# A hybrid decoder step on one core: the extra tokens' picks dealt on the core, and six expert blocks fetched into row buffers

## The chip, the cores and the metric

The kernel runs on one core of a Trainium2 chip. The metric is the device time of one execution in microseconds (us); the time of a kernel is the median of its runs. A core has five engines that run side by side, each with its own queue of instructions: TensorE (PE: matrix products, with its weight loads shown apart as PEld), VectorE (DVE), ScalarE (ACT), GpSimd (POOL) and SyncE (SP, which issues DMAs). Sixteen DMA engines move data between the memory and the on-chip SBUF. TensorE writes its results into PSUM, from which VectorE and ScalarE read.

## The reference, cut to what matters

One layer of a decoder for 272 prompt tokens (16 of them learned meta tokens) and 64 tokens of running sequences. First come a convolution branch and a state-space branch with a shared projection (the trunk). What the change touches is the expert mixer behind it:

```python
def peer_block(xb, w_q, keys, U, V):
    T = xb.shape[0]
    q = (xb @ w_q).reshape(T, PEER_HEADS, 2, D_KEY // 2)
    s = jnp.einsum('thcd,hckd->thck', q, keys).astype(jnp.float32)
    s1, i1 = lax.top_k(s[:, :, 0], PEER_TOPK)
    s2, i2 = lax.top_k(s[:, :, 1], PEER_TOPK)
    cand = (s1[..., :, None] + s2[..., None, :]).reshape(T, PEER_HEADS, PEER_TOPK * PEER_TOPK)
    sc, f = lax.top_k(cand, PEER_TOPK)
    ids = (jnp.take_along_axis(i1, f // PEER_TOPK, axis=-1) * N_KEYS
           + jnp.take_along_axis(i2, f % PEER_TOPK, axis=-1))
    g = jax.nn.softmax(sc, axis=-1)
    act = jax.nn.gelu(jnp.einsum('thkd,td->thk', U[ids], xb).astype(jnp.float32), approximate=False)
    w = (g * act).astype(xb.dtype)
    return jnp.einsum('thk,thkd->td', w, V[ids])
```

Every token picks 8 heads x 16 = 128 of 16384 experts; U and V hold 1024 numbers (4 KB) for each expert.

## The kernel before

**Three kinds of tokens.** 320 tokens go through the expert mixer (T2). 128 of them (NGAT) are "gathered": for each of their 128 picks, one indirect DMA of GpSimd fetches the picked rows of U and V for all 128 tokens at once (`gather`, L1150, 1 MB into a row buffer "wuv" of 2 x 1024 columns; there are UV = 5 such buffers), VectorE multiplies and sums (`pick_dot`, L1305), ScalarE applies the gelu and the pick's weight, and VectorE adds the weighted row of V to `ygat` (`pick_sum`, L1316). 184 tokens (ND) are "dense": their products with all experts are computed, and those that were not picked are masked out. The last 8 tokens (NX) are "extra": their 128 picks each are spread over the 128 partitions, 16 partitions to a token with 8 picks each, so that 8 further gathers serve all of them. That makes 136 gathers.

**The dense path.** U comes in 128 blocks of 512 KB. `u_block(b)` (L1416) multiplies block b with the dense tokens `nd` on TensorE (16 matmul records) and ScalarE writes the gelu into S (L1423). `g_step` (L1429) builds the mask with the weights as a product of two 0/1 matrices for 8 tokens at a time (L1449, through the two PSUM buffers "misc") and VectorE multiplies S by it (L1460). Then `v_block(b)` (L1520) multiplies the 128 blocks of V with S, and `finish` (L1496) and `finish_dense` (L1530) normalize and write the results.

**Stages and order.** The loop of the query phase (L1186) runs over 16 query halves j: a weight of w_q is loaded by SyncE (L273), cast on ScalarE (L243), its rest formed on GpSimd (L247), multiplied on TensorE (L176) and compared with the keys (L1199). Behind it run the U blocks and then the V blocks; a `Feed` hands out background tasks (picks, mask steps) at an even rate between the blocks. The framework places the instructions: each engine's order comes from a simulated schedule in which program order is the priority, so that U blocks can also fill gaps of the query phase. An engine then runs its own instructions strictly in that order, and so does SyncE with its DMA issues. Tiles of one tag in a pool share a fixed number of buffers; a new tile waits until an old one's last reader is done.

**How U blocks come in.** `fetch(i)` (L1179), called at j = 3 and j = 13, loads blocks 0 to 3 and 4 to 7 into eight places "pre" (PRE = 4 for each call). `bring` (L1386) loads the rest in order: into a ring of RING = 8 buffers of one block, which are the buffers that held the weights and their two parts before, and for blocks 16 to 23 (`again`, AGAIN = 24) into the places "pre" once more, each when the U block that was there is done. From block 24 on only the ring is left. Loads of odd blocks above LATE = 24 are issued by ScalarE, the others by SyncE (L1404). After block AGAIN - 1 the memory of the places becomes part of S (L1469).

**The extra tokens' picks.** Before, `place` (L1270) leaves ids and weights of the extra tokens in `xig`: a row for each token, which occurs in both halves of the partitions, and 64 columns (four heads) in each. `extra_columns` (L1293) deals them out by a round trip through memory: four small DMAs write `xig` to `xigd` (L1298, not before U block XW = 70 is done), a fifth reads it back as 8 columns on 128 partitions (L1301, not before block XR = 86), and VectorE copies the ids to `gid` and the weights to `ggw` (L1302, L1303). Their first use is the 65th gather.

Of the kernel before, what the change touches and what calls it, by code (L numbers as in the profile page):

```python
# [7 lines left out]
F32 = mybir.dt.float32  # L8
# [6 lines left out]
OP = mybir.AluOpType  # L15
AX = mybir.AxisListType

D = 1024
KD = 8
# [15 lines left out]
NK = 128  # L35
# [4 lines left out]
NX = 8  # L40
XQ = 128 // max(NX, 1)
ND = T2 - NGAT - NX
NPICK = 128
NCOL = NPICK + (NPICK // XQ if NX else 0)
# [8 lines left out]
SB = 84  # L53
SA = 29
PRE = 4
AGAIN = 24
HB = 64
KTILES = ((0, NGAT), (128, 128), (256, 64))
NU = (42, 26, 35)
# [4 lines left out]
RING = RB + 4  # L64
LATE = 24
OH = 2
UV = 5
# [3 lines left out]
XRES = 104  # L71
# [1 line left out]
PLACE = (42, 55)  # L73
LASTP = 126
XW = 70
XR = 86
RIGHT = "right"
TOPK = 16
EPS = 1e-6
# [38 lines left out]
def constants():  # L118
    c = np.zeros((128, NCST), np.float32)

    def put(name, a):
        o, n = CST[name]
        c[:a.shape[0], o:o + n] = a

    i = np.arange(128)
    put("ident", np.eye(128))
    put("tri", i[:, None] <= i[None, :])
    put("suf", i[:, None] > i[None, :])
    j, own, s = strips()
    n = np.arange(80)  # L130
    own = own[:, None]
    put("tri3", own & (s[j][:, None] == s[j][None, :]) & (j[:, None] <= j[None, :]))
    put("tri3n", own & (s[j][:, None] == s[None, :]) & (j[:, None] <= n[None, :]))
    put("suf3", own & (s[j][:, None] == s[j][None, :]) & (j[:, None] > j[None, :]))
    put("seg", own & (s[j][:, None] == np.arange(9)[None, :]))
    put("segs", own & (np.where(j < 64, j // 8 % 2, 2)[:, None] == np.arange(3)[None, :]))
    put("gsel", np.broadcast_to(np.arange(135) == 7, (128, 135)))
    for q in range(NQ):
        for t in range(TS):
            c[32 * (q % 4) + 8 * (q // 4) + t, CST["selq"][0] + 8 * q + t] = 1.0  # L140
    put("ones", np.ones((128, 128)))
    put("iota128", np.broadcast_to(np.arange(128), (128, 128)))
    put("sel32", i[:, None] % 32 == np.arange(32)[None, :])
    put("sel16", i[:, None] % 16 == np.arange(16)[None, :])
    put("sel8", i[:, None] % 8 == np.arange(8)[None, :])
    return c


def causal():
    m = np.zeros((128, T), np.float32)  # L150
    i, n = np.arange(128), np.arange(80)
    j, own, s = strips()
    m[:, 256:] = np.where(own[:, None] & (s[j][:, None] == s[None, :]) & (j[:, None] <= n[None, :]), 0.0, -1e30)
    for t0 in (0, 128):
        m[:, t0:t0 + 128] = np.where(i[:, None] <= i[None, :], 0.0, -1e30)
    return m


def body(tc, ia, oa, stop=None):
    nc = tc.nc  # L160
    with ExitStack() as top:
# [3 lines left out]
        dr = top.enter_context(tc.tile_pool(name="dr", bufs=1, space=bass.MemoryType.DRAM))  # L165
# [146 lines left out]
        one = dp.tile([128, 128], F32, name="one")  # L312
# [38 lines left out]
        p = misc([128, T], "pn1")  # L351
# [11 lines left out]
        t = tp.tile([128, T], F32, name="rst", tag="yo", bufs=2)  # L363
# [21 lines left out]
        r = dp.tile([H, T], F32, name="dtr")  # L385
# [547 lines left out]
        for j in range(KD):  # L933
# [4 lines left out]
            p = pj2()  # L938
# [7 lines left out]
        for j in range(KD):  # L946
            w = weight(ia["w_o"], j)
            p = pj2()
            proj(p, w, rows(mh, ml))
            x1 = xT[:, j, :T2]  # L950
# [11 lines left out]
        p = ps.tile([128, T], F32, name="pn2", tag="pb", bufs=1)  # L962
# [8 lines left out]
        gp = top.enter_context(tc.tile_pool(name="gp", bufs=1))  # L971
# [13 lines left out]
        if NX:  # L985
            x2e = gp.tile([128, D], F32, name="x2e")
            acce = gp.tile([128, D], F32, name="acce")
            xig = gp.tile([128, 2, NK // 2], F32, name="xig")
            xigd = dr.tile([XQ, NX, 2, NCOL - NPICK], F32, name="xigd")
        ks = ExitStack()  # L990
        kp = ks.enter_context(tc.tile_pool(name="kp2", bufs=1))
        qs = ExitStack()
# [8 lines left out]
        for c_ in range(2):  # L1001
            p = misc([128, 512], "px")
# [4 lines left out]
        p = misc([128, 4], "prs")  # L1007
# [140 lines left out]
        ustep, vstep = [], []  # L1148
# [19 lines left out]
            nc.gpsimd.memset(t[:, T2:], 0.0)  # L1168
        lm[0] = 0.0
        quarters[0] = 4  # L1170
        fetched = []
        pres = [ExitStack(), ExitStack()]

        pre_pools = []
# [1 line left out]
        def place_of(n):  # L1176
            return pre_pools[n // PRE].tile([128, D], F32, name="pre", tag=f"pre{n}", bufs=1)

        def fetch(i):  # L1179
            pre_pools.append(pres[i].enter_context(tc.tile_pool(name=f"pre{i}", bufs=1)))  # L1180
            for n in range(PRE):
                u = place_of(len(fetched))
                nc.sync.dma_start(u, ia["uT"][len(fetched)])
                fetched.append(u.rearrange("p (k m) -> p k m", k=KD))

        for j in range(16):  # L1186
            if j == 3:
                fetch(0)
            elif j == 13:
                fetch(1)  # L1190
            w = weight(ia["w_q"], j)
            p = pj()
            proj(p[:, :T2], w, rows(ah[:, :, :T2], al[:, :, :T2]))
            qT = qTs[j % 3]
            nc.scalar.copy(qT[:, :T2], p[:, :T2])
            p = misc([128, 3, NK], "psc")
            for i, (t0, L) in enumerate(KTILES):
                n, up = 2 * heads_of[i], 64 * (j // (2 * heads_of[i]))
                nc.tensor.matmul(p[:, i], qT[:, t0 - up:t0 - up + 128], keys[:, j, :], start=True, stop=True)  # L1199
                s_ = sall[i][:, j % n] if i else kp.tile([128, NK], F32, name="sco", bufs=9)  # L1200
                scored = nc.scalar.copy(s_[up:up + L], p[up:up + L, i]).ins.name
                if i == 0:
                    top16(sv[i], si[i], s_[:L], j)
            if j == 4:
                expert_inputs()
            if j == EXTRA - 4:
                extra_copies()
            if j == EXTRA:
                extra_tokens()
                xs.close()  # L1210
            if j == 2 * HG - 1:
                for _, f_ in heads_tasks(0):
                    f_()
            if j == 2 * HG - 1:
                ahead(0)
# [76 lines left out]

        def extra_columns():  # L1293
            m = NCOL - NPICK
            for up in (0, 64):
                src = xig[up + ND - 128:up + ND - 128 + NX].rearrange("t c (q m) -> t c q m", m=m)
                for c_ in range(2):
                    after(nc.sync.dma_start(xigd[up // m:(up + 64) // m, :, c_].rearrange("q t m -> t q m"), src[:, c_]),  # L1298
                          ustep[XW])
            back = gp.tile([128, 2, m], F32, name="xback")  # L1300
            after(nc.sync.dma_start(back, xigd.rearrange("q t c m -> (q t) c m")), ustep[XR])  # L1301
            nc.vector.tensor_copy(gid[:, NPICK:], back[:, 0])  # L1302
            nc.vector.tensor_copy(ggw[:, NPICK:], back[:, 1])  # L1303

# [69 lines left out]
        def ring():  # L1374
# [1 line left out]
            nraw[0] += 1  # L1376
            return wp.tile([128, D], F32, name="eraw", tag=tag, bufs=nb)

        coming = ([("uT", b) for b in range(2 * PRE, 128)] + [("vE", b) for b in range(XRES)] + [("x1", 0), ("x1", 5)]
                  + [("vE", b) for b in range(XRES, 128)])  # L1380
        landed, turn = {}, [0]

        def again(name, i):
            return name == "uT" and 2 * PRE + RING <= i < AGAIN

        def bring():  # L1386
            while coming:
                name, i = coming[0]
                if again(name, i):
                    if len(ustep) <= i - 2 * PRE - RING:  # L1390
                        return
                    raw = place_of(i - 2 * PRE - RING)
                else:
                    if turn[0] >= RING + used[0]:
                        return
                    raw = ring()
                    turn[0] += 1
                coming.pop(0)
                if name == "x1":
                    n = min(5, KD - i)  # L1400
                    raw = raw[:, :n * ND].rearrange("p (k t) -> p k t", t=ND)
                    nc.sync.dma_start(raw, x1d[:, i:i + n])
                else:
                    (nc.scalar if i % 2 and (name == "vE" or i > LATE) else nc.sync).dma_start(raw, ia[name][i])  # L1404
                    raw = raw.rearrange("p (k m) -> p k m", k=KD)
                landed[name, i] = raw
# [18 lines left out]
        def after(i_, name):  # L1425
            tc.add_manual_dep(i_.ins, name, mybir.DependencyInfo(mybir.DependencyClass.NoSync,
                                                                 mybir.DependencyReason.DATA), reason="paced")
# [137 lines left out]
def layout(i):  # L1565
# [24 lines left out]
    def put(name, a):  # L1590
# [17 lines left out]
        vec=vec,  # L1608
        cst=constants(),
        mneg=causal(),  # L1610
        hv=np.stack([b_in[dt0:dt0 + 32], f["dt_bias"][0], f["A_log"][0]], 1),
        w_dt=w_in[:, dt0:dt0 + 32].reshape(8, 128, 32).transpose(1, 0, 2),
        w_in=blocks(w_in[:, order]),
# [9 lines left out]
        uT=f["peer_u"][0].reshape(128, 128, 8, 128).transpose(0, 3, 2, 1).reshape(128, 128, D),  # L1623
        vE=f["peer_v"][0].reshape(128, 128, D),
# [34 lines left out]
```

## Time and profile before

| | |
|---|---|
| Median of 3 runs | 1286.79 us (1283.71 to 1288.25) |
| The profiled execution | 1286.42 us |
| Its span, first to last instruction | 1284.7 us |
| Mean granted TensorE clock | 0.991 |
| Data moved by DMA | 373.77 MB |
| Blocks of U and V | 256 x 512 KB |
| Gathers | 136, 142.62 MB, 14.7 us to land at the median |

The span has three parts in the trace: the trunk up to about 520 us, the query phase up to about 597 us, and the expert blocks, U up to 936 us and V up to 1273 us, with a tail of some 11 us behind them. In the page's rows of groups, an entry is the line, the engine, the operation, what is written and read, the count, and behind the bar the busy time, the mean of one in ns, and the engine's idle time before it with what ended it. A row of the timeline has the start and the duration in us, and in brackets the idle time before it with its releaser. A row of the windows has from:to, the length, then the busy time and count of PE, PEld, DVE, ACT and POOL, the granted clock (1.00 is full speed), the mean busy share of the DMA engines, and GB/s. A row of the waits has who waited for whom, the sum in us, how often, and the longest.

### The profile page before, as it was taken

Reading aid. Unit: us, or ns where it says so; the run is one execution under the profiler, and the core shown is the slowest. Engines: PE = TensorE matmul, PEld = TensorE weight load, DVE = VectorE, ACT = ScalarE, POOL = GpSimd, SP = SyncE. Lnnn points to the kernel's source line nnn. Section 1 sums busy time; section 2 is a strip of 40 time slices with the busy share of each in tenths; the row PEclk is TensorE's granted clock in tenths of the full one; section 3 lists DMA queues with packets and bytes.
Section 4 is the critical chain, followed back from the end, with each engine's and each line's share of the span. In section 5 each row is a group of like instructions: output and inputs, shape, how many; then the busy total and the mean of one; then the engine's idle time right before and its main releaser. Section 6 shows DMA issues by size and latency. Waiting matters only on the chain.

```text
span 1284.7 us, 23645 instructions
## 1 busy us (share of the span) xinstructions
PE 1260.9 (98%) x8951; PEld 1217.3 (95%) x8951; DVE 961.1 (75%) x2119; ACT 520.3 (40%) x1308; POOL 600.3 (47%) x595
## 2 busy tenths in 40 slices
PE   9999999999999999999999998999999999999997
PEld 7989999999889999999999998999999999999997
DVE  6888889888977345449999977878887887545555
ACT  6778777878676444544232221222211101001102
POOL 2487787887795757974132222133333322122210
PEclk9899999999999999999999999999999999999999
DMA  6435455445334444766989999999999999999994
GB/s 248 168 124 193 160 186 184 142 157 180 139 125 146 161 150 146 270 214 248 375 321 415 416 414 415 408 408 409 412 415 414 416 415 415 399 415 414 414 415 175
DMA packets 85905, 373.77 MB, mean 291 GB/s; under 512 B 10000, under 2 KB 15376, under 8 KB 66208
## 3 DMA queue, kind: packets, MB, share of 16 engines
q1 hardware_dynamic: 48336, 166.82, 35.1%
q0 software_dynamic: 19584, 142.62, 27.3%
q10 hardware_dynamic: 17872, 62.84, 12.2%
q8 instruction: 70, 1.15, 0.4%
q14 instruction: 43, 0.35, 0.1%
HBM read 359.18 MB, written 13.06 MB: 290 GB/s over the span
## 4 chain that ended last, share of the span: by engine, by line
PE 76%; DVE 11%; DMA 8%; issue 2%; POOL 1%; ACT 1%; ACTq 0%; POOLq 0%; SPq 0%; DVEq 0%
PE pj L176 32%; PE va L1523 23%; PE pj L1421 13%; DMA wuv<-in_peer_uv_dram,gid 4%; DMA eraw<-in_uT_dram 3%; DVE ygat L1319 2%; PE pg L1449 2%; DVE wuv L1309 1%; DVE pcv L519 1%; PE pst L176 1%; DMA eraw<-in_vE_dram 1%; PE po L176 1%; PE py L176 1%; PE pq L176 1%; DMA wdt<-in_w_dt_dram 1%
## 5 line engine op out<-in xcount | busy, mean ns | idle before, releaser
L1152 POOL DMA_INDIRECT wuv<-in_peer_uv_dram,gid x136 | 170.6, 1254 | 481.8 <-PE va L1523 121.7
L247 POOL TENSOR_TENSOR wl<-wraw,wh 128x256 fp32r<-128x256 f32 (+1 forms) x202 | 290.3, 1456 | 109.3 <-ACT wh L243 64.7
L1523 PE MATMUL va<-S,eraw 128*128 128x184 f32 x2048 | 325.5, 320 | 0.0
L1523 PEld LDWEIGHTS va<-S,eraw 128*128 128x128 f32 x2048 | 318.9, 190 | 1.1 <-issue 0.9
L1421 PE MATMUL pj<-nd,eraw 128*128 128x184 f32 x1792 | 292.8, 323 | 6.5 <-DMA eraw<-in_uT_dram 5.7
L1421 PEld LDWEIGHTS pj<-nd,eraw 128*128 128x128 f32 x1792 | 281.1, 191 | 7.6 <-ACT scg L1311 4.8
L176 PE MATMUL pj<-ah,wh 128*128 128x336 f32 (+1 forms) x768 | 242.7, 327 | 1.6 <-ACT xg L219 1.2
L176 PE MATMUL pj<-al,wh 128*128 128x336 f32 (+1 forms) x768 | 232.5, 316 | 0.0
L1319 DVE SCALAR_TENSOR_TENSOR ygat<-wuv,scg,ygat 128x1024 f32<-128x1024 f32 x128 | 164.1, 1282 | 76.9 <-ACT scg L1314 76.8
L1311 ACT ACTIVATE scg<-scg 128x1 f32<-128x1 f32 x136 | 27.3, 202 | 418.2 <-DVE wuv L1309 269.9
L1309 DVE SCALAR_TENSOR_TENSOR wuv<-wuv,x2m 128x1024 f32<-128x1024 f32 x128 | 156.1, 1220 | 43.5 <-DMA wuv<-in_peer_uv_dram,gid 43.3
L243 ACT CAST wh<-wraw 128x1024 fp32r<-128x1024 f32 x125 | 131.0, 1049 | 78.4 <-PE pj L176 55.7
L176 PEld LDWEIGHTS pj<-ah,wh 128*128 128x128 f32 x768 | 145.6, 190 | 7.1 <-issue 2.7
L176 PEld LDWEIGHTS pj<-al,wh 128*128 128x128 f32 x768 | 145.2, 190 | 0.7
L176 PE MATMUL pj<-ah,wl 128*128 128x336 f32 (+1 forms) x768 | 138.5, 315 | 1.9 <-POOL wl L247 1.9
L519 DVE SCALAR_TENSOR_TENSOR pcv<-ch,vec,pcv 128x320 f32<-128x320 f32 x232 | 127.6, 550 | 10.8 <-ACT pcv L517 8.1
L176 PEld LDWEIGHTS pj<-ah,wl 128*128 128x128 f32 x768 | 120.2, 188 | 3.0 <-POOL wl L247 2.9
L1423 ACT ACTIVATE S<-pj 128x184 f32<-128x184 f32 x128 | 38.3, 317 | 115.7 <-PE pj L1421 115.4
L530 DVE SCALAR_TENSOR_TENSOR pj<-mcat,vec,pj 128x360 f32<-128x360 f32 x96 | 56.4, 590 | 5.5 <-ACT pj L528 5.1
L1460 DVE SCALAR_TENSOR_TENSOR S<-pg,S 128x232 f32<-128x232 f32 (+1 forms) x92 | 34.6, 418 | 34.2 <-PE pg L1449 34.1
L1314 ACT ACTIVATE scg<-scg,ggw 128x1 f32<-128x1 f32 x136 | 39.7, 294 | 6.7 <-PE va L1523 2.6
L1421 PE MATMUL pj<-nd,pre 128*128 128x184 f32 x256 | 42.0, 319 | 0.0
(388 smaller groups left out, 1696.0 us busy)
## 6 DMA issues: line engine op xcount, KB each, us to landing
wraw<-in_w_in_dram SPq DMA_DIRECT2D x80, 512.0 KB, 3.2
eraw<-in_vE_dram SPq DMA_DIRECT2D x64, 512.0 KB, 10.0
eraw<-in_vE_dram ACTq DMA_DIRECT2D x64, 512.0 KB, 10.4
eraw<-in_uT_dram SPq DMA_DIRECT2D x60, 512.0 KB, 9.6
eraw<-in_uT_dram ACTq DMA_DIRECT2D x52, 512.0 KB, 9.5
st<-in_state_dram SPq DMA_DIRECT2D x8, 1024.0 KB, 4.8
out_ssm_s_dram<-st SPq DMA_DIRECT2D x8, 1024.0 KB, 4.2
wraw<-in_w_mo_dram SPq DMA_DIRECT2D x16, 512.0 KB, 3.2
```

The lines of the kernel that those rows point to most:

```text
L176: i_ = nc.tensor.matmul(*a_, **kw)
L243: (nc.vector.tensor_copy if on_dve else nc.scalar.copy)(h, src)
L247: (nc.gpsimd if on_pool else nc.vector).tensor_tensor(l[:, q:q + m], src[:, q:q + m], h[:, q:q + m].bitcast(F32), op=OP.subtract)
L519: nc.vector.scalar_tensor_tensor(to, in_, sc, eights(acc), op0=OP.mult, op1=OP.add)
L530: nc.vector.scalar_tensor_tensor(o, cat[:, w:w + n], wv, o, op0=OP.mult, op1=OP.add)
L1152: i_ = nc.gpsimd.indirect_dma_start(out=u, out_offset=None, in_=ia["peer_uv"], in_offset=bass.IndirectOffsetOnAxis(ap=gid[:, c:c + 1], axi ...
L1309: nc.vector.scalar_tensor_tensor(u[:, :D], u[:, :D], 1.0, x2m if c < NPICK else x2e, op0=OP.mult, op1=OP.mult, accum_out=w)
L1314: nc.scalar.activation(w, w, AF.Copy, scale=ggw[:, c:c + 1])
L1319: nc.vector.scalar_tensor_tensor(a_, u[:, D:], scg[:, c:c + 1], a_, op0=OP.mult, op1=OP.add)
L1421: i_ = nc.tensor.matmul(p[:, :ND], raw[:, k, :], nd[:, k, :], start=(k == 0), stop=(k == KD - 1))
L1423: nc.scalar.activation(Sv(b), p[:, :ND], AF.Gelu)
L1523: i_ = nc.tensor.matmul(va[k // 2][:, k % 2], raw[:, k, :], Sv(b), start=(b == 0 and k % 2 == 0), stop=(b == 127), skip_group_check=True)
```

## The change

Two things are done.

The extra tokens' picks no longer go through memory. A constant `xsel` (128 x 136 numbers, a new input loaded in the query phase) holds a 0/1 matrix that copies, for each of the 128 partitions, the right row of `xig` (128 columns), and a 0/1 mask that says which 8 of the 64 columns belong to the partition (8 columns). `extra_columns` multiplies `xig` by the first on TensorE into a "misc" buffer of PSUM (not before U block XW = 70), VectorE multiplies the result by the mask and sums over the 8 groups of columns. The two copies behind it stay.

Blocks 0 to 5 of U are loaded in the query phase, at j = 5, 7 and 9, two to a row buffer of the gathers, so three of the five "wuv" buffers hold U blocks until these are used. The eight places "pre" then hold blocks 6 to 13 (still called at j = 3 and 13), the ring starts at block 14 (FIRST), and blocks 22 to 28 are loaded into "pre" again (AGAIN = SA = 29).

```diff
-AGAIN = 24
+FETCH = (5, 7, 9)
+ROWS = len(FETCH)
+FIRST = 2 * ROWS + 2 * PRE
+AGAIN = SA
...
-XR = 86
...
+def extra_places():
+    r, p = np.arange(128)[:, None], np.arange(128)[None, :]
+    row = 64 * (p // NX // (XQ // 2)) + ND - 128 + p % NX
+    mine = np.arange(XQ // 2)[None, :] == (np.arange(128) // NX % (XQ // 2))[:, None]
+    return np.concatenate([(r == row), mine], 1).astype(np.float32)
...
-            xigd = dr.tile([XQ, NX, 2, NCOL - NPICK], F32, name="xigd")
+            xsel = gp.tile([128, 128 + XQ // 2], F32, name="xsel")
+            nc.sync.dma_start(xsel, ia["xsel"])
...
-        fetched = []
+        fetched = {}
...
+        def fetch_to(b, u):
+            nc.sync.dma_start(u, ia["uT"][b])
+            fetched[b] = u.rearrange("p (k m) -> p k m", k=KD)
+
         def fetch(i):
             pre_pools.append(pres[i].enter_context(tc.tile_pool(name=f"pre{i}", bufs=1)))
-            for n in range(PRE):
-                u = place_of(len(fetched))
-                nc.sync.dma_start(u, ia["uT"][len(fetched)])
-                fetched.append(u.rearrange("p (k m) -> p k m", k=KD))
+            for n in range(PRE * i, PRE * i + PRE):
+                fetch_to(2 * ROWS + n, place_of(n))
+
+        def fetch_rows(n):
+            u = gp.tile([128, 2 * D], F32, name="wuv", bufs=UV)
+            for a in range(2):
+                fetch_to(2 * n + a, u[:, a * D:a * D + D])
 
         for j in range(16):
             if j == 3:
                 fetch(0)
+            elif j in FETCH:
+                fetch_rows(FETCH.index(j))
             elif j == 13:
                 fetch(1)
...
         def extra_columns():
             m = NCOL - NPICK
-            for up in (0, 64):
-                src = xig[up + ND - 128:up + ND - 128 + NX].rearrange("t c (q m) -> t c q m", m=m)
-                for c_ in range(2):
-                    after(nc.sync.dma_start(xigd[up // m:(up + 64) // m, :, c_].rearrange("q t m -> t q m"), src[:, c_]),
-                          ustep[XW])
+            p = misc([128, 2, NK // 2], "pxi")
+            after(nc.tensor.matmul(p.rearrange("p c j -> p (c j)"), xsel[:, :128], xig.rearrange("p c j -> p (c j)"),
+                                   start=True, stop=True), ustep[XW])
+            one = gp.tile([128, 2, XQ // 2, m], F32, name="xone")
+            nc.vector.tensor_tensor(one, p.rearrange("p c (q m) -> p c q m", m=m),
+                                    xsel[:, None, 128:, None].to_broadcast([128, 2, XQ // 2, m]), op=OP.mult)
             back = gp.tile([128, 2, m], F32, name="xback")
-            after(nc.sync.dma_start(back, xigd.rearrange("q t c m -> (q t) c m")), ustep[XR])
+            nc.vector.tensor_reduce(back, one.rearrange("p c q m -> p c m q"), axis=AX.X, op=OP.add)
             nc.vector.tensor_copy(gid[:, NPICK:], back[:, 0])
             nc.vector.tensor_copy(ggw[:, NPICK:], back[:, 1])
...
-        coming = ([("uT", b) for b in range(2 * PRE, 128)] + [("vE", b) for b in range(XRES)] + [("x1", 0), ("x1", 5)]
+        coming = ([("uT", b) for b in range(FIRST, 128)] + [("vE", b) for b in range(XRES)] + [("x1", 0), ("x1", 5)]
...
         def again(name, i):
-            return name == "uT" and 2 * PRE + RING <= i < AGAIN
+            return name == "uT" and FIRST + RING <= i < AGAIN
...
                 if again(name, i):
-                    if len(ustep) <= i - 2 * PRE - RING:
+                    n = i - FIRST - RING
+                    if len(ustep) <= 2 * ROWS + n:
                         return
-                    raw = place_of(i - 2 * PRE - RING)
+                    raw = place_of(n)
```

More of the change, by code (lines that the diff above doesn't have):

```diff
@@ L1610, in layout @@
         mneg=causal(),
+        xsel=extra_places(),
         hv=np.stack([b_in[dt0:dt0 + 32], f["dt_bias"][0], f["A_log"][0]], 1),
```

## The prediction

> **What bounds the kernel now.** First the page: busy shares and slices.
>
> ```profile
> PE 1260.9 (98%) x8951; PEld 1217.3 (95%) x8951; DVE 961.1 (75%) x2119; ACT 520.3 (40%) x1308; POOL 600.3 (47%) x595
> GB/s 248 168 124 193 160 186 184 142 157 180 139 125 146 161 150 146 270 214 248 375 321 415 416 414 415 408 408 409 412 415 414 416 415 415 399 415 414 414 415 175
> ```
>
> Two things are full together. TensorE is busy for 98% of the span, and from the 22nd slice on (a slice is 32.1 us, so from about 674 us) the DMA engines move some 415 GB/s and seldom less. At that rate a 512 KB block (524,288 bytes) takes 1.26 us. TensorE can lose only the time in which it stands still or runs slowly, so I next read its waits from 480 us on, and where they lie in its timeline.
>
> ```profile
> PE pj L1421 <- DMA eraw<-in_uT_dram: 5.7, 2, 4.5
> PE pj L1421 <- ACT S L1423: 0.7, 1, 0.7
> ...
> 690.70 10.28 PE L1421 MATMUL pj<-nd,eraw 128*128 128x184 f32 x64 [1.16 <-DMA eraw<-in_uT_dram]
> 726.90 8.09 PE L1421 MATMUL pj<-nd,eraw 128*128 128x184 f32 x48 [0.67 <-ACT S L1423]
> ...
> 791.02 2.74 PE L1421 MATMUL pj<-nd,eraw 128*128 128x184 f32 x16
> 798.28 5.25 PE L1421 MATMUL pj<-nd,eraw 128*128 128x184 f32 x16 [4.52 <-DMA eraw<-in_uT_dram]
> ```
>
> There are three pauses, 6.35 us in all, and the one at 798.28 is most of it. The same 16 matmuls of a block take 2.74 us before that pause and 5.25 us behind it. The windows around it say why:
>
> ```profile
> 797.00:798.28 1.28, 0.00 (x1) 0.03 (x1) 1.28 (x4) 0.38 (x2) 0.17 (x1) 0.50 1.03 419
> 802.00:803.84 1.84, 1.84 (x15) 1.69 (x15) 0.19 (x2) 0.28 (x2) 0.00 (x0) 0.50 1.01 414
> 803.84:806.00 2.16, 2.16 (x24) 2.16 (x22) 1.77 (x5) 0.43 (x3) 0.00 (x0) 1.00 1.03 423
> ```
>
> The granted clock is 0.50 from 797.00 to 803.84. Of that, TensorE works from 798.28 on: 5.56 us at half speed, 2.78 us lost. The pause thus costs 4.52 + 2.78 = 7.30 us. [...]
>
> Why was the block late? SyncE's DMA queue, its waits from 765 to 785 us, the chain's own piece, and the usual time to land:
>
> ```profile
> 769.76 7.78 SPq L1298 DMA_DIRECT2D xigd<-xig  x4
> 777.64 42.93 SPq L1404 DMA_DIRECT2D eraw<-in_uT_dram  x8
> ...
> SPq L1298 <- DMA eraw<-in_uT_dram: 6.5, 2, 4.1
> SPq L1404 <- DMA xigd<-xig: 2.3, 1, 2.3
> ...
> 777.64 20.50 DMA eraw<-in_uT_dram
> ...
> eraw<-in_uT_dram SPq DMA_DIRECT2D x60, 512.0 KB, 9.6
> ```
>
> The four little writes of the extra tokens' picks (L1298) held SyncE's queue for 7.78 us, nearly all of it waits for landings. The block load queued behind them left at 777.64 and took 20.50 us to land, where the median is 9.6. It landed at 798.14, and TensorE started at 798.28.
>
> **The change part by part.**
>
> *The product in place of the round trip through memory* removes four writes and one read, all on SyncE. The block behind them leaves up to 7.78 us earlier and lands up to 20.50 - 9.6 = 10.9 us sooner after that. Together that is more than the 4.52 us by which it was late, so this pause goes, and with it the half clock: **-4.52 and -2.78**. The next thing late would be the following ordinary block. The stretch from 700 to 790 ran on the same ring of eight with one pause of 0.67, so I leave nothing for it here and keep it as a rival. Added: one f32 matmul with 128 columns, one multiply that reads 128 columns from PSUM, and one sum over those 128 columns. Their nearest rows:
>
> ```profile
> L1044 PE MATMUL px<-cst,wuv x8: 270/272/273, 570.4 to 574.0; 128*128 128x128 f32 x8
> L1460 DVE SCALAR_TENSOR_TENSOR S<-pg,S x92: 316/417/515, 765.3 to 1097.1; 128x232 f32<-128x232 f32 x23, 128x280 f32<-128x280 f32 x23, 128x160 f32<-128x160 f32 x23, 128x352 f32<-128x352 f32 x23
> ```
>
> On TensorE that is two such records, so 0.3 to 0.55 us on the path; I take **+0.3**, since matmuls overlap. On VectorE it is at most twice the 0.316 us of the smallest L1460 form (160 columns): 0.2 to 0.6 us. The product of each pick hides it, which waits for gathers in that stretch (the DMA is full): nothing. Without that cover it would delay one pick's sum by 0.6 us. The matmul also takes one of the two "misc" buffers in PSUM that the L1449 products rotate through, until VectorE has read it; what is queued behind it on TensorE are U blocks that need no such buffer. Bounds 0 and 1 us; I take 0. Loading xsel (128 x 136 numbers, 70 KB) is 0.2 us of DMA in the query phase.
>
> *Blocks 0 to 5 in row buffers.* Every block of U is still loaded once, so the number of loads stays. What moves is when. Before:
>
> ```profile
> 531.64 10.57 SPq L273 DMA_DIRECT2D wraw<-in_w_q_dram  x3
> 542.31 1.80 SPq L1183 DMA_DIRECT2D pre<-in_uT_dram  x4
> ...
> 577.00 20.24 SPq L1404 DMA_DIRECT2D eraw<-in_uT_dram  x8
> 599.85 11.64 SPq L1404 DMA_DIRECT2D pre<-in_uT_dram  x5
> ...
> L1404 SPq DMA_DIRECT2D pre<-in_uT_dram x8: 327/328/328, 551.7 to 611.2; - x8
> ...
> 530.00:540.00 10.00, 10.00 (x72) 10.00 (x71) 7.40 (x17) 7.68 (x18) 10.00 (x12) 1.00 0.98 381
> 570.00:580.00 10.00, 9.74 (x71) 9.33 (x69) 4.43 (x19) 6.38 (x15) 9.71 (x13) 1.00 0.33 111
> 630.00:667.00 37.00, 37.00 (x240) 37.00 (x239) 37.00 (x119) 9.39 (x30) 12.25 (x10) 1.00 0.88 326
> ```
>
> Eight blocks of U first go into "pre" (four of them at 542.31). Eight more are loaded into the same places, each as soon as its place is free; of those, five were still to come at 599.85. So by then 8 first loads, 3 reloads and 8 blocks in the ring were under way: 19 blocks. After the change it is 6 in rows + 8 + 8 = 22, with no reload before 600, since the places are now those of blocks 6 to 13. That is three blocks more, **3.8 us of DMA lead** (bounds 0, if the gap at 570 to 580 isn't used, and 6 x 1.26 = 7.6). Behind that the ring is eight deep in both, so the lead can be kept only where the DMA had room, as between 630 and 667 (326 of 415 GB/s: 7.9 us). The pause at 690.70 came from a block 1.16 us late in full traffic; a lead of 3.8 covers it: **-1.16** (bounds -1.16 and 0). The 0.67 behind ScalarE I keep.
>
> What can this cost? SyncE issues the six loads between the weights of the query heads, and what is queued behind them is the next weight, for which ScalarE's cast, GpSimd's split and then TensorE wait. The window 530 to 540 is full already at 381 GB/s. Per pair of blocks a weight is 2.5 us later. Bounds: 0, as later heads find two thirds of the DMA free at 570 to 580 and U blocks can stand in, and 7.6, if all six stand before one weight. TensorE stands only 0.26 us between 570 and 580 now; nearer to that end I take **+1.0**. The row buffers are also those of the gathers; with three of five held until block 5 is done, the first gathers (at 598.7) may wait a few us, on VectorE, which is full there with the picking anyway: 0.
>
> Sum on TensorE: -4.52 - 2.78 + 0.3 - 1.16 + 1.0 = **-7.2 us**.
>
> *Does the end follow?* The end has a second side: gathers, then the last rows.
>
> ```profile
> 1271.12 0.37 ACTq L1518
> 1271.85 0.33 ACT sqd L1535
> ...
> 820.00:840.00 20.00, 20.00 (x167) 19.78 (x165) 16.55 (x30) 4.47 (x16) 6.00 (x5) 1.00 1.01 402
> 840.00:860.00 20.00, 20.00 (x166) 19.65 (x165) 16.10 (x31) 3.92 (x15) 5.62 (x5) 1.00 1.01 403
> 860.00:880.00 20.00, 20.00 (x160) 19.77 (x159) 16.89 (x31) 4.26 (x15) 7.23 (x5) 1.00 1.01 405
> 1100.00:1120.00 20.00, 20.00 (x131) 20.00 (x130) 10.06 (x12) 1.84 (x8) 3.15 (x4) 1.00 1.00 389
> ```
>
> The finish of the gathered tokens ends on ScalarE at 1271.49, and the dense finish starts at 1271.85: only 0.36 us apart. The gathers can end earlier only by what the DMA engines save: the lead of 3.8 and the room they had behind 800. That is, from the GB/s that lack to 415, (13 + 12 + 10)/415 x 20 = 1.7 us in the first three windows and 26/415 x 20 = 1.3 in the last. So 3.8 + 3.0 = 6.8, plus 0.36 before they decide: 7.2. Both sides give the same.
>
> The profiled execution took 1286.42 us (span 1284.7 and 1.7 around it), 0.37 below the median of 1286.79. So 1286.42 - 7.2 = 1279.2 for such an execution, and **1279.6** for a median.
>
> **Rivals.**
>
> - *The bytes decide.* No lead comes of the fetches, TensorE saves its 7.2 us, but the gathers end only 3.0 + 0.36 = 3.4 us sooner: 1283.4. For it: the GB/s row is flat at 415. Against it: two thirds of the DMA lie idle at 570 to 580. [...]
> - *The pause comes back* elsewhere between 660 and 820, since the ring is as deep as before and the gathers keep the queues full. At 4.5 us and half clock again the change is worth 0 to -1: 1286.3. For it: a pause of 1.16 at 690 with no xigd near it. Against it: 20.50 us to land is the largest of all block loads.
> - *The weights starve* (slower). If the six row loads and the four of 542.31 stand together in SyncE's queue before one weight, it is 10 x 1.26 = 12.6 us late. TensorE then stands up to that long and runs at half clock behind it: 12.6 + 2.8 = 15.4 in place of my 1.0, against a gain of 8.2 without it: +7.2, so 1294.0. It decides from about 5.4 us of standing still (5.4 + 2.8 = 8.2). For it: 530 to 540 is full. Against it: the loads come in three pairs at three heads.
> - *The change doesn't do what it says*: the row loads leave only with the ring's at 577. Then the product's part stands alone: no lead, but no late weight either. TensorE would save 7.0, the gathers 3.4, so 1283.4, as with the bytes.
>
> **How the numbers follow.** Forecast 0.55; the bytes 0.12 and the idle fetch 0.05 (both 1283.4); the returning pause 0.18; starving 0.10. About 0.3% (3.9 us) is what a measurement of this kernel can tell from no change. Faster by more: all of the forecast and half of 1283.4, **0.63**; slower by more: **0.10**; within: **0.27**. Low end: all three pauses gone at no cost, -4.52 - 2.78 - 1.83 + 0.3 = -8.8, so 1278.0, and 2 us for the scatter of the runs (1283.71 to 1288.25): 1276. High end: the returning pause and a little for scatter, 1287.5; starving is left out.
>
> **What would show it.** Right: no xigd in SyncE's queue; no pause of TensorE above 1 us from 660 to 820 and a clock of 1.00 there; 22 blocks of U under way by 600; the last rows' finish and the dense finish both some 7 us earlier. Wrong: a pause ended by "DMA eraw" in 660 to 820 (returning pause); a gap between the last V product and the dense finish (the bytes); TensorE idle before 600 behind the casts or GpSimd's split (starving).

## The result, and the profile after

The changed kernel takes 1278.74 us (median of 4 runs, 1276.94 to 1280.32), against 1287.37 for the kernel before in the same rounds: 8.6 us less, a ratio of 0.993 with a 95% interval of 0.9914 to 0.9946 (-7.0 to -11.1 us). The profiled execution took 1279.01 us, with a span of 1277.2. First the page of after: the slices of DMA rate, and below them TensorE's only wait between 480 us and the end of the V products.

```profile
GB/s 247 166 130 190 162 190 167 140 178 170 143 129 149 149 150 149 293 226 211 323 385 391 420 419 421 420 421 421 419 421 420 421 420 418 401 420 421 419 421 147
...
PE pj L1442 <- DMA eraw<-in_uT_dram: 1.0, 1, 1.0
```

Two things are to be seen. The waits of 5.7 and 0.7 us are down to 1.0. And the flat stretch from the 23rd slice on reads 418 to 421 GB/s where before it read 408 to 416 (but for one slice in each, and the last); nothing that the prediction counted explains a faster flat stretch. That row turned out to matter. Next, the timeline of TensorE at the pause that is left, the windows over the place of the old pause, and the timeline of SyncE's queue:

```profile
726.42 7.72 PE L1442 MATMUL pj<-nd,eraw 128*128 128x184 f32 x48 [0.95 <-DMA eraw<-in_uT_dram]
...
797.00:806.00 9.00, 9.00 (x72) 8.94 (x71) 8.35 (x18) 2.06 (x10) 2.75 (x2) 1.00 1.02 422
...
639.46 189.19 SPq L1425 DMA_DIRECT2D eraw<-in_uT_dram  x34
```

TensorE is busy for all 9.00 us of 797 to 806 at clock 1.00; before, that stretch held the last 1.28 us of the pause, and the clock was 0.50 until 803.84. SyncE issues 34 block loads in one row, with no other write among them. The early fetch, in the timelines of SyncE and GpSimd, did only part of what it says:

```profile
532.25 0.90 SPq L1190 DMA_DIRECT2D wuv<-in_uT_dram  x2
...
534.29 1.61 SPq L1190 DMA_DIRECT2D wuv<-in_uT_dram  x2
...
603.17 0.86 SPq L1190 DMA_DIRECT2D wuv<-in_uT_dram  x2
...
601.38 0.94 POOL L1162 DMA_INDIRECT wuv<-in_peer_uv_dram,gid  x1 [0.30 <-issue]
619.76 0.94 POOL L1162 DMA_INDIRECT wuv<-in_peer_uv_dram,gid  x1 [17.44 <-PE pj L1442]
```

Two pairs leave at 532 and 534, the third only at 603.17, behind the fourth gather (601.38): in the order of the program four gathers take row buffers before j = 9 does. So by 600 there are 4 + 8 + 8 = 20 blocks under way, one more than before, not three. The end, as the chain of waits has it:

```profile
1233.65 20.60 DMA wuv<-in_peer_uv_dram,gid
...
1261.37 0.73 ACT wraw L1535
...
1262.19 1.73 POOLq L1677
1263.94 0.37 ACTq L1539
...
1264.67 0.33 ACT sqd L1556
```

Here the last gather and the rows' finish decide the end (1264.67, 7.18 us before the 1271.85 of the kernel before). In a second profile of the same kernel (d0_after) it began behind the V products instead, as the timeline's bracket says:

```profile
1263.63 0.32 ACT L1556 ACTIVATE sqd<-va 128x184 f32<-128x184 f32 x1 [4.29 <-PE va L1544]
```

The two sides are still within a microsecond or two of each other. TensorE's own side, the end of the V products in the timelines of before and of after:

```profile
1254.78 18.85 PE L1523 MATMUL va<-S,eraw 128*128 128x184 f32 x119
```

```profile
1254.72 10.76 PE L1544 MATMUL va<-S,eraw 128*128 128x184 f32 x68
```

They end at 1273.63 before and at 1265.48 after, 8.15 us earlier.

### The profile page after: what moved, and what is told of

Its sections match the earlier page's. It is cut to its first block, busy times and chain, and to the rows that moved or that the text cites. A ratio compares the mean times of both kernels' runs of the same rounds, so it can differ in the third digit from the quotient of the medians.

```text
span 1277.2 us, 23639 instructions
## 1 busy us (share of the span) xinstructions
PE 1259.0 (99%) x8953; PEld 1215.0 (95%) x8953; DVE 964.0 (75%) x2121; ACT 520.2 (41%) x1308; POOL 604.9 (47%) x595
## 4 chain that ended last, share of the span: by engine, by line
PE 79%; DVE 13%; DMA 4%; POOL 1%; ACT 1%; issue 1%; POOLq 0%; ACTq 0%; DVEq 0%
PE pj L185 32%; PE va L1544 23%; PE pj L1442 15%; DMA wuv<-in_peer_uv_dram,gid 3%; DVE ygat L1339 2%; DVE wuv L1329 2%; PE pg L1470 2%; DVE pcv L528 1%; PE pst L185 1%; PE py L185 1%; PE po L185 1%; DMA eraw<-in_uT_dram 1%; PE pq L185 1%; DMA wdt<-in_w_dt_dram 1%; POOL st L690 1%
## 5 line engine op out<-in xcount | busy, mean ns | idle before, releaser
L1162 POOL DMA_INDIRECT wuv<-in_peer_uv_dram,gid x136 | 175.5, 1290 | 470.1 <-DVE oh L1466 101.8
L1442 PE MATMUL pj<-nd,eraw 128*128 128x184 f32 x1712 | 277.0, 321 | 1.0 <-DMA eraw<-in_uT_dram 1.0
L1442 PEld LDWEIGHTS pj<-nd,eraw 128*128 128x128 f32 x1712 | 266.4, 190 | 1.3 <-ACT scg L1331 1.2
L1339 DVE SCALAR_TENSOR_TENSOR ygat<-wuv,scg,ygat 128x1024 f32<-128x1024 f32 x128 | 164.0, 1281 | 66.5 <-ACT scg L1334 63.5
```

What stands on the lines that cost most here:

```text
L1162: i_ = nc.gpsimd.indirect_dma_start(out=u, out_offset=None, in_=ia["peer_uv"], in_offset=bass.IndirectOffsetOnAxis(ap=gid[:, c:c + 1], axi ...
L1339: nc.vector.scalar_tensor_tensor(a_, u[:, D:], scg[:, c:c + 1], a_, op0=OP.mult, op1=OP.add)
L1442: i_ = nc.tensor.matmul(p[:, :ND], raw[:, k, :], nd[:, k, :], start=(k == 0), stop=(k == KD - 1))
```

## The experiments

Theory 1: the four small writes in SyncE's queue make the pause at 798, and the product takes it away. Rival 1: the blocks fetched early, and the lead they give. Rival 2: bytes decide, so TensorE's gain doesn't reach the end. From the second group on, a third question stood beside them: where do the 5 GB/s come from? All ratios are to the kernel before, run beside each kernel on the same chip.

| kernel | median us | ratio (95%) | GB/s behind 700 us |
|---|---|---|---|
| after, again (d0_after) | 1277.79 | 0.9928 (0.9914 to 0.9941) | 420 |
| c2_product | 1279.75 | 0.9939 (0.9925 to 0.9952) | 420 |
| c3_rows | 1286.59 | 0.9988 (0.9979 to 0.9997) | 415, 394 to 410 behind the trip |
| c4_early | 1277.89 | 0.9917 (0.9903 to 0.993) | 420 |
| d1_trip | 1284.74 | 0.9984 (0.9974 to 0.9993) | 420, 414 for some 100 us behind the trip |
| d2_onewrite | 1278.13 | 0.9936 (0.9921 to 0.9951) | 420 |
| e1_input | 1288.72 | 0.999 (0.9974 to 1.0005) | 420, 405 to 413 behind the trip |
| e2_onchip | 1279.16 | 0.9909 (0.9886 to 0.9933) | 420 |
| e3_tile | 1287.26 | 0.9981 (0.9965 to 0.9997) | 420, 400 to 414 behind the trip |
| f1_shift | 1287.77 | 0.998 (0.9966 to 0.9993) | 415 |
| f2_align | 1290.58 | 0.9998 (0.9987 to 1.0009) | 415 |

### The two parts alone

c1_before is the kernel before, unchanged.

> The kernel before once more, profiled on the chip of the runs beside it. If the two profiles differ only by the kernels: the pause of TensorE behind a late block near 798 us is there again (4 to 5 us, with half clock behind it), and the DMA engines move 413 to 416 GB/s behind 660 us where the profile of after had 419 to 421. If part of the gain is a difference between chips or executions: 419 GB/s or more here too, or no pause above 1 us near 798.

One execution took 1285.78 us and has the pause again (timeline of TensorE):

```profile
796.59 4.98 PE L1421 MATMUL pj<-nd,eraw 128*128 128x184 f32 x16 [4.29 <-DMA eraw<-in_uT_dram]
```

The windows from 680 to 780 read 413 to 415 GB/s. Neither the pause nor the rate is an accident of one execution.

c2_product is the kernel before with the product only:

```diff
-                    after(nc.sync.dma_start(xigd[up // m:(up + 64) // m, :, c_].rearrange("q t m -> t q m"), src[:, c_]),
...
+            after(nc.tensor.matmul(p.rearrange("p c j -> p (c j)"), xsel[:, :128], xig.rearrange("p c j -> p (c j)"),
```

> The product alone: the kernel before with the extra tokens' picks dealt by the product, no U blocks in row buffers. Theory 1 (the pause at 798 and its half clock came from the four small writes in SyncE's queue): -7.0 us, so about 1280; the pauses at 690 (1.2) and 727 (0.7) stay, none near 798. Rival 1 (the gain comes from the U blocks fetched early, and the lead they give): 0 to -1 us, a pause of 3 us or more stays between 760 and 820. Rival 2 (bytes decide): TensorE saves 7, but the gathers end only 3.4 us sooner, so -3.4.

-7.9 us (0.9939). The waits of TensorE:

```profile
PE pj L1430 <- DMA eraw<-in_uT_dram: 0.8, 1, 0.8
PE pg L1458 <- DVE S L1469: 0.3, 1, 0.3
```

The pause near 798 is gone, and so is that at 690, without any early fetch. Nearly the whole gain is there, but c2 also holds the new tile `xsel`, which matters below. Rival 2, which ought to have held it at -3.4, did not, and the rate is 420.

c3_rows is the kernel after with the round trip put back (the reverse of the edit above).

> The early fetch alone: the kernel after with the round trip through memory put back. Theory 1: SyncE's queue is held again for some 7.8 us at the small writes, the pause of 4 to 5 us with half clock comes back between 760 and 820; only the 1.16 at 690 is saved: 0 to -1.2 us against before, about 1286. Rival 1 (early fetch and lead): the block behind the writes comes in time, -7 us, about 1280. In between (-2 to -5): one block of lead (1.26 us) shortens the pause and the two parts overlap.

-1.5 us (0.9988). The pause is back at its full size, behind the same four writes; the wait's name is that of a ScalarE instruction that shares it (timeline, then windows):

```profile
797.88 5.25 PE L1441 MATMUL pj<-nd,eraw 128*128 128x184 f32 x16 [4.62 <-ACT scg L1333]
...
780.00:800.00 20.00, 15.38 (x108) 14.89 (x107) 16.71 (x30) 3.31 (x14) 5.03 (x5) 0.92 1.02 417
800.00:820.00 20.00, 20.00 (x156) 19.67 (x155) 13.05 (x23) 3.14 (x13) 2.67 (x3) 0.91 1.01 410
```

Rival 1 falls. The early fetch alone is worth about the pause at 690.

### How much the third pair of blocks is worth

```diff
-FETCH = (5, 7, 9)
+FETCH = (5, 6, 7)
```

> The kernel after with FETCH = (5, 6, 7), so that the third pair of U blocks gets its row buffer ahead of the first gathers. My step as predicted (22 blocks under way by 600, 3.8 us of lead where the kernel after has one block, 1.26): the six loads leave before 545, the 5th gather leaves some 10 us sooner than 619.8, the 0.95 us pause at 726 goes, and the time is 1 to 3 us below after. Rival (the lead is lost again where the ring waits, behind 630): within 0.5 us of after. Rival (weights starve): TensorE stands 1 us or more between 530 and 600, 0 to 3 us slower than after.

0.9917 against 0.993 and 0.9928 of after: the intervals overlap, so a gain over after (0.0011 of the time, 1.4 us, against d0_after) isn't settled. The order did come out as the prediction had wanted it (timelines of SyncE and GpSimd): 22 blocks under way by 600, and the fifth gather at 607.69.

```profile
532.23 2.55 SPq L1190 DMA_DIRECT2D wuv<-in_uT_dram  x4
...
538.22 0.81 SPq L1190 DMA_DIRECT2D wuv<-in_uT_dram  x2
...
607.69 0.94 POOL L1162 DMA_INDIRECT wuv<-in_peer_uv_dram,gid  x1 [2.00 <-PE pj L1442]
...
701.38 10.21 PE L1442 MATMUL pj<-nd,eraw 128*128 128x184 f32 x64 [0.94 <-DMA eraw<-in_uT_dram]
```

Yet a pause of 0.94 is there, only earlier, and the last gather leaves at 1234.05 against 1233.65 in after: three blocks of lead at 600 move nothing at the end.

### The writes by themselves

d1_trip is the kernel after with four writes and a read that nobody uses; d2_onewrite has one write instead:

```diff
+            xout = dr.tile([128, 2, NK // 2], F32, name="xout")
+            after(nc.sync.dma_start(xout, xig), ustep[XW])
```

> The kernel after with a round trip through memory that nobody uses: the same four small writes behind U block 70 and the read back behind block 86; the columns themselves still come from the product. Theory 1 (the hold of SyncE's queue by these writes makes the pause): the pause of 4 to 5 us with half clock is back near 790, +5.5 to +8 us against after, about 1285 to 1287. Rival (the product itself, its place in the order or the new input saves the time): the pause does not come back, within 1 us of after. On the DMA rate, which was 414 to 416 GB/s in the runs with the round trip and 419 to 421 in those without it: 415 here if the trip or its memory makes the difference, 420 if the new input does (its place in memory shifts the others).

> The kernel after with one write in place of four: the whole of xig, 128 rows of 512 bytes, goes to a tensor in memory that nobody reads, on SyncE behind U block 70. If it is the number of writes (four wait for one another's landings, and later loads for theirs): one write holds the queue for at most 4 us, no pause above 1 us near 790, 0 to +1 us against after. If any write to memory in the saturated stage holds the queue: a pause of 3 us or more near 790, +4 to +7. On the DMA rate: 415 GB/s if a tensor in memory or any write makes the difference, 420 if the four small writes or the read back do.

> The kernel after once more, on the chip of the runs beside it, as the mark for them: 1278 to 1280 us, 419 to 421 GB/s, one pause of about 1 us near 726, none near 790.

d1 costs 1284.74 - 1277.79 = 7.0 us against d0, d2 costs 0.3. SyncE's queue in d1, TensorE behind it, and the same places in d2:

```profile
769.10 7.41 SPq L1318 DMA_DIRECT2D xigd<-xig  x4
776.60 39.76 SPq L1433 DMA_DIRECT2D eraw<-in_uT_dram  x8
...
796.77 2.73 PE L1450 MATMUL pj<-nd,eraw 128*128 128x184 f32 x16 [3.67 <-DMA eraw<-in_uT_dram]
```

```profile
768.62 0.38 SPq L1315 DMA_DIRECT2D xout<-xig  x1
773.19 55.10 SPq L1427 DMA_DIRECT2D eraw<-in_uT_dram  x11
```

The queue is held for 7.41 us as before (7.78), and the late block makes a pause of 3.67. The profiled execution of d1 is the fastest of its twelve (1282.18), and in it the clock stayed at 1.00 behind the pause; the others are some 2.6 us longer, near the 2.78 that half clock cost in before; that they ran at half clock is an estimate, as no profile of them was taken. So the hold, and not the product or its place, carries Theory 1. One write of 64 KB does no harm. The read back can't make this pause: it leaves at 816.46 (timeline of SyncE in d1), 20 us behind it. Whether it is the number of the writes or their small pieces was not separated.

### Where the 5 GB/s come from

The runs with 420 GB/s had the new input; those with 415 had not. But its tile also moves what lies behind it in SBUF by 544 bytes in each partition. e2_onchip is the kernel after with the same tile filled on VectorE and no input; e1_input is the kernel before with the input loaded and unused; e3_tile is the kernel before with the tile alone, filled by a copy of the identity. The edit of e2_onchip:

```diff
-            nc.sync.dma_start(xsel, ia["xsel"])
+            nc.vector.tensor_copy(xsel[:, :128].rearrange("r (h g t) -> r h g t", h=2, t=NX),
+                                  ident.rearrange("r (h x) -> r h x", h=2)[:, :, None, ND - 128:ND - 128 + NX].to_broadcast([128, 2, XQ // 2, NX]))
+            nc.vector.tensor_reduce(xsel[:, 128:], ident.rearrange("p (h g t) -> p g h t", h=2, t=NX), axis=AX.XY, op=OP.add)
```

> The kernel after without the new input: the same 0/1 matrix and mask, in the same tile of SBUF, are made on VectorE from the identity that is there already. So far every run with the input moved 419 to 421 GB/s behind 674 us and every run without it 414 to 416, with or without the round trip. Theory 3 (the new input shifts what lies in memory, and that sets the rate): 415 GB/s here, the gathers end up to (421 - 415) / 415 x 560 = 8 us later than in after, and the time is 1280 to 1285. Rival (the product, or the tile's place in SBUF, sets it): 420 GB/s, 1277 to 1279.5.

> The kernel before with the new input loaded into a tile that nobody reads; the round trip stays. Theory 3 (input): 420 GB/s from 674 us on, the pause near 798 stays, and since TensorE sets the end, the gain is small: 0 to -2 us. Theory 3b (place of later tiles in SBUF): 420 too, and then the run with the tile alone moves 420 as well. Rival (what reads the matrix, not the load of it): 415 GB/s, within 0.5 us of before.

> The kernel before with the tile of 128 x 136 numbers in SBUF alone, filled on VectorE from the identity, with no input: later tiles of its pool lie 544 bytes further on in each partition. Theory 3 (input): 414 to 416 GB/s. Theory 3b (place in SBUF): 419 to 421. Time by either: within 2 us of before, as the pause near 798 stays.

The input falls: without it, e2 and e3 move 420, and e1, which loads it for nothing, gains nothing clear of noise (0.999). (One of e2's six executions took 4845.28 us, which nothing here explains; the ratio leaves it out.) e3 has the old round trip, the old loads and no input; it differs from before by an SBUF tile and its fill. Its slices, and the chain at its end:

```profile
GB/s 251 164 126 193 160 186 183 141 158 181 138 135 133 158 154 148 250 233 222 378 323 417 421 420 420 418 400 411 414 421 419 417 420 420 376 422 420 419 421 151
...
1224.85 46.45 PE va L1525 x298
1271.30 0.02 issue
1271.32 0.33 ACT sqd L1537
```

The rows' finish of the gathered tokens starts at 1265.41, 3.1 us earlier than in before (1268.55), and the chain at the end is V products alone: the time is -2.5 us (0.9981), since the pause of TensorE is still there. But the last gather leaves as late as in before, behind a V product (timelines of GpSimd in before, after and e3):

```profile
1241.65 1.84 POOL L1152 DMA_INDIRECT wuv<-in_peer_uv_dram,gid  x1 [3.59 <-PE va L1523]
```

```profile
1233.65 1.27 POOL L1162 DMA_INDIRECT wuv<-in_peer_uv_dram,gid  x1 [3.70 <-PE va L1544]
```

```profile
1241.33 1.13 POOL L1154 DMA_INDIRECT wuv<-in_peer_uv_dram,gid  x1 [4.05 <-PE va L1525]
```

The code says why: `gather` holds each gather back until a block a few steps earlier is done (the dependency "rows after blocks", LEAD = 4). By the matmul records, the last gather leaves at the same point of TensorE's work in all three runs, with 115 blocks of V and 6 matmuls of the next begun. So a TensorE that is 8 us earlier lets the gathers leave 8 us earlier; a higher rate alone does not.

f1_shift takes the shift away from the kernel after: its input, its product, its loads, but row buffers that begin where the rate was 415, 32 past a multiple of 64.

```diff
-            xsel = gp.tile([128, 128 + XQ // 2], F32, name="xsel")
+            xsel = gp.tile([128, 136 + XQ // 2], F32, name="xsel")[:, :128 + XQ // 2]
...
-            back = gp.tile([128, 2, m], F32, name="xback")
+            back = gp.tile([128, 3, m], F32, name="xback")[:, :2]
```

> The kernel after with one change of place: the tile of the 0/1 matrix is 8 numbers (32 bytes) wider, so the gathers' five row buffers begin at 32 bytes past a multiple of 64, as in every run that moved 414 to 416 GB/s; in every run with 419 to 421 they begin at a multiple of 64. (The tile xback is widened too, so that all later tiles move by 64.) Theory 3b (place of the row buffers): 415 GB/s behind 700 us, though input and product are those of after. Then the worth of the rate is seen: if the gathers set the end (the rival that the bytes decide), their finish comes up to 7 us later and the time is 1281 to 1285; if the lead alone would do, as the prediction had it, within 1 us of after, 1277.5 to 1279.5. Rival to 3b: 420 GB/s, and the place isn't it.

0.998: of the 0.7% of after, 0.2% is left. (Its 1287.77 us lie above the 1281 to 1285 that were expected, beside a kernel before that took 1289.90.) Its slices, and the chain at its end:

```profile
GB/s 249 175 133 175 173 174 183 155 157 182 128 143 128 156 156 140 322 190 251 315 355 416 415 414 415 414 415 415 414 416 414 415 414 415 400 414 416 413 416 124
...
1242.50 21.25 DMA wuv<-in_peer_uv_dram,gid
...
1270.87 0.73 ACT wraw L1535
1271.63 0.07 issue
1271.70 1.73 POOLq L1677
```

There is no pause near 798, but the last gather leaves at 1242.50, as late as in before (1241.65) and 8.85 us later than in after; 117 blocks of V have begun by then, two more than in after, so here it isn't TensorE that holds it. It leaves 0.77 us behind the sum on VectorE that frees its row buffer (`ygat`, done at 1241.73), just as the gather before it does, and VectorE had waited 3.46 us for the rows of that sum. The gathers and the rows' finish are the chain. TensorE doesn't keep its gain either (its timeline):

```profile
789.04 0.67 PE L1470 MATMUL pg<-oh 128*128 128x64 f16 x7 [1.50 <-DVE oh L1466]
...
854.06 0.50 PE L1470 MATMUL pg<-oh 128*128 128x64 f16 x11 [1.44 <-DVE S L1481]
...
1262.37 11.91 PE L1544 MATMUL va<-S,eraw 128*128 128x184 f32 x64 [3.04 <-DMA eraw<-in_vE_dram]
```

After has none of the three. Ahead of the first two VectorE had itself stood 1.77 and 1.95 us for gathered rows (at 783.80 and 852.10), and behind the third the clock is 0.50 for 3.41 us. This is Rival 2, bytes decide: the gain of 7 us doesn't reach the end.

The gathers' own queue shows the cost. The queue rows of before, after and f1 have packets, MB, and the time that their packets took as a share of the span of 16 engines:

```profile
q0 software_dynamic: 19584, 142.62, 27.3%
```

```profile
q0 software_dynamic: 19584, 142.62, 26.9%
```

```profile
q0 software_dynamic: 19584, 142.62, 27.2%
```

Times the spans, that is 0.273 x 1284.7 = 350.7 us, 0.269 x 1277.2 = 343.6 and 0.272 x 1286.8 = 350.0, for the same bytes: 6 to 7 us. From 1215 to 1260 us the queue's share of 16 x 45 us comes to 38.0 to 38.2 us of one engine for a MB in after, c2, c4, d1 and e3, and to 38.8 to 38.9 in before, c3, f1 and f2. In the traces' records behind 700 us the 8 KB packet of a gather takes 309 ns at the median in after and 315 in before; the 4 KB packet of a block load takes 159 or 160 in both.

f2_align is c4_early with the constants' tile and that of the matrix each 32 bytes wider. It was meant to be the version that beats both.

> The kernel c4_early with 8 unused numbers behind the constants, and the tile of the 0/1 matrix 8 numbers wider: now the ring's eight buffers, which begin at 32 past a multiple of 64 in every run so far, begin at a multiple of 64, and the row buffers still do. Theory 3b, if it holds for the block loads as for the gathers: more than 421 GB/s, about 425, the pause near 701 gone, and 0 to -2 us against c4_early, as TensorE stands still for only 1.1 us there: 1276 to 1278. Rival (only the gathers' writes feel it): 420 GB/s, 1277 to 1278.5.

It lost everything: 415 GB/s, 0.9998. So a multiple of 64 is not the point. Where the row buffers begin, in bytes of a partition, read from the placement of the built programs (no trace holds it; the steps from row to row follow from the edits, 544 bytes for the tile and 32 and 64 more):

| runs | row buffers begin at | past a multiple of 64 | of 128 | of 256 | GB/s |
|---|---|---|---|---|---|
| before, c1, c3 | 78560 | 32 | 96 | 224 | 415 |
| f1 | 79136 | 32 | 32 | 32 | 415 |
| f2 | 79168 | 0 | 64 | 64 | 415 |
| after, c2, c4, d0 to d2, e1 to e3 | 79104 | 0 | 0 | 0 | 420 |

A multiple of 128 or of 256 fits all runs. Why the place counts was not shown; measured is the 8 KB packet, which takes 315 ns in before and 309 in after, 2% less. The ring's buffers (18336, in f2 18368) were never at such a multiple, so no run shows what the place does to a block load. What stays open: 128 or 256, and whether the distance of the row buffers from the ring (a multiple of 64 in all runs with 415, 32 beside one in those with 420) plays a part. No run tells these apart, and a ring at a multiple of 256 wasn't tried.

## Why the prediction was right, and where by luck

Predicted were 1279.6 us, measured 1278.74. TensorE's sum was -7.2; the V products ended 8.15 us earlier, 1 us more, as the +1.0 for late weights came to nothing. That the dense finish came just 7.18 us earlier is luck: the gathered rows held it in that execution, and in d0_after it started at 1263.63, 8.2 us earlier. The steps, one by one:

- *The pause at 798, -4.52 and -2.78*: right, cause and size. It goes with the writes (c2), comes back with them (c3 at 4.62 with half clock, d1), and d1 costs 7.0 us. Nothing took its place.
- *The pause at 690, -1.16*: gone, but c2 has none there either, so the lead isn't needed for it. The 0.67 at 727 became 0.95.
- *The product's own cost, +0.3 on TensorE, nothing on VectorE*: right. By the profile's records matmuls do overlap: in before one of a U block takes 323 ns at the mean, and 16 take 2.74 us. The instructions of the tile "pxi" in after:

```profile
L1315 PE MATMUL pxi<-xig,xsel x2: 275/314/352, 847.4 to 847.6; 128*128 128x128 f32 x2
L1318 DVE TENSOR_TENSOR xone<-pxi,xsel x1: 280/280/280, 851.0 to 851.0; 128x128 f32<-128x128 f32 x1
```

  Half a microsecond there, and in c2 a wait of TensorE of 0.3 behind VectorE, inside the bounds.
- *Weights late, +1.0*: nothing. TensorE is busy in full through the query phase (windows of after):

```profile
530.00:540.00 10.00, 10.00 (x72) 9.90 (x71) 7.47 (x16) 7.59 (x18) 10.00 (x12) 1.00 1.04 402
540.00:550.00 10.00, 10.00 (x73) 9.79 (x72) 4.29 (x24) 3.74 (x9) 9.92 (x12) 1.00 1.03 418
...
570.00:580.00 10.00, 10.00 (x68) 9.30 (x67) 3.79 (x20) 6.97 (x17) 8.65 (x11) 1.00 0.31 105
```

- *"22 instead of 19 blocks", a lead of 3.8 us*: mis-sized. It was 20 blocks, one block of 1.26 us, since the third pair stood behind four gathers for a row buffer. The prediction counted the five buffers and overlooked who takes them first. With 22 (c4) the end hardly moves.
- *"The gathers can end earlier only by what the DMA engines save: the lead of 3.8 and the room they had behind 800"*: this step failed. The last gather did leave 8.0 us earlier (1241.65 to 1233.65), but from neither lead nor room: f1 has both, and its last gather leaves at 1242.50. The prediction overlooked that a gather waits for a block of TensorE. In before, after and e3 the last one leaves at the same point of the V products, so it was TensorE's gain of 8 us that brought it forward. The DMA engines decide whether that can be kept: at 420 GB/s it was, at 415 (f1) the gathers fell two blocks behind. And the rate rose because the new tile moved the row buffers to a better place (from 78560 to 79104), which the prediction didn't have. f1, which lacks only that, shows what the prediction's own edits bring without it: 0.998 (0.9966 to 0.9993). The rival "the bytes decide" stood at 1283.4, a ratio of 0.9974, inside that interval. It had a chance of 0.12 and was right about 415 GB/s: at that rate the gathers' end gains next to nothing, though TensorE loses its gain there too, where the rival let it keep 7.2.

So the number came true in part by luck. TensorE's gain was predicted with its cause; that it reaches the gathers, and the rate that lets it through, were not. Each alone is worth little (product and fetch without the shift, f1: 0.998; the shift without the product, e3: 0.9981); together they give 0.993. That is how two bounds behave that lie 0.36 us apart at the end: the time follows the later one.

## What to carry to other kernels

Where two sides end together, price them as two separate sums with separate causes, and give the side that is flat at a rate no gain unless a step names what frees its bytes; then test by taking away one side's gain alone. Read in the code, too, which dependencies tie one side to the other. A change that adds a tile moves every tile behind it (by 544 bytes here): compare the flat part of the DMA rate before and after, and if it moved, look at where the DMA's targets begin before crediting the edit. Small transfers through memory in the queue that feeds a saturated ring cost more here than their bytes (7.41 us of hold in d1 for four writes of 2 KB), and the product on the core was cheaper (-7.9 us in c2); for buffers shared by tag, count who asks first in the order of the program.

## What the hardware showed that was not expected

- A gather into row buffers that begin at 79104 takes 309 ns for each 8 KB packet (after); at 78560 it takes 315 (before), and 32 or 64 bytes behind 79104 a MB costs 38.9 or 38.8 us of one engine (f1, f2) where it costs 38.1 in after. Over 136 gathers that is 6 to 7 us of all 16 DMA engines, 415 against 420 GB/s.
- Block loads behind the small writes waited for the writes' landings, though they share no data. The waits of SyncE's queue in before, from 690 to 830 us:

```profile
SPq L1404 <- DMA xigd<-xig: 6.3, 2, 4.0
```

  In the trace of before the 333 DMAs of SyncE and the 125 of ScalarE use eight completion semaphores in turn, and each waits until the last user of its own has landed; the four writes took four of the eight from 769.76 to 777.28. The one that left at 772.85 landed at 789.80, and the next load with its semaphore left at 790.95.
- The half clock comes in pieces of about 3.41 us (before: 6.83 at 42.66, 3.41 at 363.51, 6.83 at 797.01), and not by the pause's length alone: 6.83 us of it at pauses of 2.63 (f2, 1265 us), 3.87 (e1), 4.29, 4.52 and 4.62, 3.41 at 3.04 (f1, 1262 us), 3.27 (f2) and 4.15 (e3), none at 3.49 (e1) and 3.67 (d1).
